# Four of twelve column pairs of a feed-forward's way up as seven half-size products, with the weight sums made by adding transfers

## The chip, the cores and the metric

The kernel runs on one core of one Trainium2 chip. Its five engines work side by side, each through its own queue in order: TensorE (PE in the profile; its weight loads are the row PEld) multiplies, VectorE (DVE) and ScalarE (ACT) do elementwise work and empty PSUM, the accumulators that TensorE writes, GpSimd (POOL) and SyncE (SP) here mostly issue transfers (DMAs) between the main memory (HBM) and SBUF, the working memory. The metric is the device time of one execution in microseconds (us), the median over the runs of a kernel.

## The reference

One batch, 512 tokens, width 1024, two layers, float32. Layer 0 mixes tokens by dilated window attention (24 heads in three groups), layer 1 by a gated linear recurrence (RG-LRU). Each is followed by a gated feed-forward with a causal convolution over three tokens, and each sub-layer is wrapped in two RMS norms.

```python
def conv_ffn(x, w_up, conv_w, conv_b, w_down):
    u = causal_dwconv(x @ w_up, conv_w, conv_b)
    g, v = u[..., :D_FF], u[..., D_FF:]
    return (jax.nn.gelu(g, approximate=True) * v) @ w_down

for layer in range(DEPTH):                     # DEPTH = 2, D_FF = 3072
    h = rms_norm(x, norm_mix_pre[layer])
    h = dilated_attention_mixer(h, ...) if layer % 2 == 0 else rglru_mixer(h, ...)
    x = x + rms_norm(h, norm_mix_post[layer])
    h = rms_norm(x, norm_ffn_pre[layer])
    h = conv_ffn(h, ffn_w_up[layer], ffn_conv_w[layer], ffn_conv_b[layer], ffn_w_down[layer])
    x = x + rms_norm(h, norm_ffn_post[layer])
```

## The kernel before

**Numbers in two parts.** Every large product takes both operands as a rounded high part and the rest, the low part, and is made of three matmuls: high by high, high by low, low by high (`mm3`, line 326). A weight piece is split by one ACT copy (`hi`, line 215, in `pump`) and one DVE subtraction (`lo`, line 226, in `low_parts`). The normed activations stand transposed in `hT`: a high and a low tile of 128 partitions x 8 blocks of features x 512 tokens.

**Weights.** `plan` lists all weight pieces in the order of use. `loads` issues the next one on SP's queue as long as fewer than `RAW_BUFS` = 3 raw buffers of 1 MB are in use (`load`, line 253). `pump` takes the next piece of a landed or coming load and splits it, as long as fewer than `W_UNITS` = 8 split pieces are live; the low part of the previous piece follows the high part of the next, and the last low part of a load frees its raw buffer. `tick` is called after each output tile; it runs the waiting side steps (norms, softmax steps) and the pump. So the program order of every engine is fixed when the kernel is built, by these ticks.

**A feed-forward.** `ffn` walks over 12 pairs of column blocks. For pair j, `feat_tiles` makes two tiles of 128 gate columns and two of 128 value columns, each 8 feature blocks x 3 matmuls over 512 tokens, so a pair is 96 matmuls and 2 MB of weights. Pair 0 runs in token halves, 192 matmuls over 256 tokens. `sink` empties a tile: `conv` makes the first tap on ACT (line 600) and two on DVE (line 604); a gate tile goes through gelu on ACT (line 615), a value tile is multiplied into it on DVE (line 619). `rows_run` then makes the way down token tile by token tile into accumulators, and starts for each finished tile the two norms, `postnorm` (which updates the residual `xs_sb[t]`) and `prenorm` (which makes the next `hT`).

**Half-size products that are there already.** In the attention the value columns of the second and third head group are made by seven products of half size (`value_steps`) in place of eight: sums of corners of `hT` (`sums`, lines 739 to 745, one set for each of two groups of columns) times sums of quarters of the weights (`added`, line 236, on DVE, from raw buffers that are held meanwhile), combined on DVE (line 788).

**GpSimd's queue** loads the bias strips (`toe`, line 666), the norms' gains (line 160) and the small column constants (`columns`, line 551). The gains' tile (`gain`) is also the place of the weight sums. The residual x keeps four tiles of the tag `x` through the whole layer, beside the token sums in the attention.

Of the kernel before, what the change touches and what calls it, by code (L numbers as in the profile page):

```python
# [18 lines left out]
P = 128  # L19
# [14 lines left out]
RAW_BUFS = 3  # L34
# [3 lines left out]
WARM = 14  # L38

# [46 lines left out]
def kernel(  # L86
# [61 lines left out]
    def load_x(t, cuts=1):  # L148
        xt = htp.tile([P, D], F32, tag="x", name=nm("x"), bufs=4)
        n = D // cuts  # L150
        for i in range(cuts):
            c = slice(i * n, (i + 1) * n)
            nc.sync.dma_start(xt[:, c], x[0, t * P : (t + 1) * P, c])
        return xt
# [13 lines left out]
    state = {"dma": 0, "cv": 0, "live": 0, "next": 0, "read": 0, "rows": False, "hold": False}  # L168
# [3 lines left out]
    total = {}  # L172

    def parts_of(kind, raw):

        if kind == "feat":
            return [raw[:, :, m * P : (m + 1) * P] for m in range(2)]
        if kind == "held":
            total["held"] = raw
            return []  # L180
        if kind in ("value", "sum0", "sum"):
            return [raw[:, 2 * i : 2 * i + 2, :] for i in range(2)]
        if kind == "rows":
            return [raw[:, i : i + 1, :] for i in range(2)]
        return [raw]

    def pump(limit=2, now=False):

        for _ in range(limit):
# [4 lines left out]
            if pieces and state["live"] < W_UNITS:  # L194
                i, j, raw = pieces.pop(0)
                last = not pieces
                if plan[i][0] in ("sum0", "sum"):
                    raw = added(plan[i][0], j, raw)
                    if last:
                        state["read"] += 1 + (plan[i][0] == "sum0")  # L200
                        last = False
# [3 lines left out]
                if i < 2 or now:  # L205
# [7 lines left out]
                    state["read"] += last  # L213
# [10 lines left out]
    def low_parts():  # L224
        for _, _, lo, raw, hi, last in late:
            nc.vector.tensor_tensor(lo, raw, hi.bitcast(F32), op=ALU.subtract)  # L226
            state["read"] += last
        late.clear()

    def added(kind, j, raw):  # L230

        if kind == "sum0" and j == 0:
            total["sum"] = cp.tile([P, 4, 512], F32, tag="gain", name=nm("sum"))
        h = slice(2 * j, 2 * j + 2)
        part = total["sum"][:, h, :]
        nc.vector.tensor_tensor(part, total["held"][:, h, :] if kind == "sum0" else part, raw, op=ALU.add)
        return part

    def loads():
        while state["dma"] < len(plan) and state["dma"] - state["read"] < RAW_BUFS:  # L240
            load()

    def load():
        i = state["dma"]
        kind, kd, cols, srcs = plan[i]
        raw = wp.tile([P, kd, cols], F32, tag="raw", name=nm("raw"), bufs=RAW_BUFS)
        at = 0
        for src, n in srcs:
            if i < 2:
                for k in (0, 2):  # L250
                    nc.sync.dma_start(raw[:, k : k + 2, :], src[:, k : k + 2, :])
            else:
                nc.sync.dma_start(raw[:, :, at : at + n] if kd == 4 and cols == 512 else raw[:, at : at + n, :], src)
# [9 lines left out]
    def take(i, j):  # L263
        while (i, j) not in units:
            before = state["live"]
            pump(1, True)
            assert before != state["live"]
# [51 lines left out]
    def w_rows(w, r0):  # L319
        plan.append(("rows", 2, D, [(w[r0 : r0 + 256, :].rearrange("(k p) c -> p k c", p=P), 2)]))  # L320
# [109 lines left out]
    def norms(t, banks, post_g, pre_g, hT):  # L430
        state["hold"] = t >= 2
        postnorm(t, banks, post_g, hT is None)
        if hT is not None:
            yield from prenorm(t, hT, pre_g, 3 if t == 3 else 4)
        if t == 3:
            state["hold"] = False

# [10 lines left out]
    def feat_tiles(n, hT, sink, halves=False):  # L448
# [15 lines left out]
        for c in range(n):  # L464
            i = chunk()
            for m in range(2):
# [4 lines left out]
                tick()  # L471

    def rows_proj(nchunks, act, order, post, pre):
# [12 lines left out]
        def run():  # L486
            return rows_run(nchunks, A, prep, seq, order, post, pre)
# [3 lines left out]
    def rows_run(nchunks, A, prep, seq, order, post, pre):  # L491
# [7 lines left out]
        for tiles, chunks in order:  # L499
            for c in chunks:  # L500
# [9 lines left out]
                for n, part in enumerate(loop):  # L510
# [17 lines left out]
                    for t in tiles:  # L528
                        if left[t] == [0, 0]:
                            side(norms(t, banks[t], post_g, pre_g, hT))  # L530
# [14 lines left out]
    def columns(parts):  # L545
# [4 lines left out]
        for src, c in parts:  # L550
            nc.gpsimd.dma_start(st[at : at + c, :P], src)
# [43 lines left out]
    def ffn(layer, hT, post, pre):  # L595
# [13 lines left out]
        gv = []  # L609

        def sink(b, ps, j):
            m = b % 2
            if b < 2:
                u = conv(ps, 2 * j + m)
                nc.scalar.activation(u, u, AF.Gelu_apprx_tanh)  # L615
                gv.append(u)
# [3 lines left out]

        order = [([0, 1, 2, 3], range(9)), ([0], range(9, 12)), ([1], range(9, 12))]
# [9 lines left out]
    def attention(hT, post, pre):  # L631
# [84 lines left out]
        def sums(n):  # L716

            def cut(i, j, h):
                return hT[h][:, 4 * i : 4 * i + 4, j * 256 : (j + 1) * 256]

            made, run = {}, []
            terms_of = {
                3: [((1, 1), 1), ((0, 1), -1)],
                2: [((0, 0), 1)],
                4: [((1, 0), -1)],
                1: [((0, 1), 1), ((0, 0), -1)],
            }

            def make(*names):
                for name in names:  # L730
                    if name in (3, 1):
                        run[:] = [gp.tile([P, 4, 256], F32, tag="run", name=nm("run"), bufs=1)]
                    hi, lo = (htp.tile([P, 4, 256], F32R, tag="x", name=nm("T"), bufs=4) for _ in range(2))
                    made[name] = hi, lo
                    r = run[0]
                    parts = [(cut(*ij, x).bitcast(F32), sg) for ij, sg in terms_of[name] for x in range(2)]
                    if name in (3, 1):
                        (a, _), (b, _) = parts[:2]
                        nc.vector.tensor_tensor(r, a, b, op=ALU.add)
# [577 lines left out]
```

## Time and profile before

| | |
|---|---|
| median of 3 runs | 1480.87 us (1480.69 to 1481.19) |
| the profiled execution | 1480.85 us, with a span of 1479.1 us from its first to its last instruction |
| engines busy in the span | PE 99%, DVE 58%, ACT 42%, POOL 2% |
| granted TensorE clock, mean | 0.997 |
| DMA | 174.40 MB, mean 118 GB/s |
| matmuls | 7049 |

The page gives for each engine the time in which one of its instructions ran. Matmuls overlap in the pipeline, so the length of one in a group (some 390 ns over 512 columns) is not its price; the price is the distance from one to the next. The view of windows adds up busy time within stretches, the view of waits says what ended the idle time of an engine, and the chain of waits is followed back from the last instruction to whatever released it. "SPq" is SP's queue.

### The profile page before, as it was taken

The page shows a single profiled execution, that of the slowest core. Times are in us where ns is not written, and L with a number is a line of the kernel's source. Part 1 is how long each engine was busy: PE and PEld are TensorE (multiplying, and loading weights), DVE is VectorE, ACT ScalarE, POOL GpSimd, SP SyncE. Part 2 cuts the span into 40 slices and gives each one's busy share as a digit, 9 for nine tenths or more (in the row PEclk, how much of TensorE's full clock was granted, in tenths as well). Part 3 has the DMA queues.
Part 4 walks back from the last instruction along what each step waited for, and adds up shares of the span by engine and source line. Part 5 has one row for each costly group of instructions (what it writes and reads, how often), then busy time and mean ns, then how long its engine had stood idle before and what let it go on. Part 6 is the DMA issues. An engine that isn't in the chain of part 4 may idle for free.

```text
span 1479.1 us, 17722 instructions
## 1 busy us (share of the span) xinstructions
PE 1466.7 (99%) x7049; PEld 1232.1 (83%) x7049; DVE 856.0 (58%) x1459; ACT 623.2 (42%) x1042; POOL 34.2 (2%) x67
## 2 busy tenths in 40 slices
PE   8999999999999999999999999999999999999998
PEld 6788888888888898888888888988898888888886
DVE  5366746684455676555565337778775555565333
ACT  5344333343435453334344234579453333333221
POOL 0121000000000000000000000000000000000000
PEclk9999999999999999999999999999999999999999
DMA  6545354636326143232223321341323232323201
GB/s 224 202 174 166 120 177 158 202 127 223 107 90 217 35 137 114 86 110 90 93 107 116 112 86 44 100 143 57 123 92 114 87 113 86 105 95 121 107 0 57
DMA packets 129714, 174.40 MB, mean 118 GB/s; under 512 B 5775, under 2 KB 108391, under 8 KB 129632
## 3 DMA queue, kind: packets, MB, share of 16 engines
q1 hardware_dynamic: 124736, 162.02, 32.7%
q0 software_dynamic: 4896, 11.26, 2.3%
q8 instruction: 55, 0.90, 0.3%
q14 instruction: 27, 0.22, 0.1%
HBM read 164.82 MB, written 13.14 MB: 120 GB/s over the span
## 4 chain that ended last, share of the span: by engine, by line
PE 97%; DVE 1%; DMA 1%; ACT 1%; SPq 0%; issue 0%; DVEq 0%
PE ps L326 59%; PE acc L326 23%; PE vq L757 5%; PE v L697 3%; PE gate L326 1%; PE tr L375 1%; PE S L932 1%; PE O L903 1%; PE S L868 1%; DMA raw<-in_attn_w_qkv_dram 1%; PE O L1000 1%; PE PT L890 0%; PE PT L981 0%; DVE wlo L226 0%; ACT L L920 0%; PE OT L1004 0%
## 5 line engine op out<-in xcount | busy, mean ns | idle before, releaser
L326 PE MATMUL ps<-hT,whi 128*128 128x512 f32 (+1 forms) x2752 | 802.0, 376 | 0.0
L326 PEld LDWEIGHTS ps<-hT,whi 128*128 128x128 f32 x2752 | 502.7, 188 | 93.1 <-ACT qk L677 0.6
L326 PE MATMUL ps<-hT,wlo 128*128 128x512 f32 (+1 forms) x1376 | 515.2, 374 | 0.0
L226 DVE TENSOR_TENSOR wlo<-raw,whi 128x1024 fp32r<-128x1024 f32 x244 | 295.5, 1219 | 130.0 <-ACT whi L215 129.5
L215 ACT ACTIVATE whi<-raw 128x1024 fp32r<-128x1024 f32 x244 | 253.2, 1052 | 136.6 <-PE acc L326 124.4
L326 PEld LDWEIGHTS ps<-hT,wlo 128*128 128x128 f32 x1376 | 259.0, 188 | 46.4
L604 DVE SCALAR_TENSOR_TENSOR u<-ps,cols,u 128x511 f32<-128x511 f32 x192 | 143.8, 749 | 217.1 <-ACT u L600 213.7
L326 PE MATMUL acc<-whi,ahi 128*128 128x512 f32 x512 | 200.4, 391 | 0.0
L326 PE MATMUL acc<-whi,alo 128*128 128x512 f32 x512 | 199.3, 389 | 0.0
L326 PE MATMUL acc<-wlo,ahi 128*128 128x512 f32 x512 | 199.2, 389 | 0.0
L600 ACT ACTIVATE u<-ps,cols 128x512 f32<-128x512 f32 x96 | 74.8, 779 | 220.0 <-PE ps L326 215.6
L326 PEld LDWEIGHTS acc<-whi,alo 128*128 128x128 f32 x512 | 96.1, 188 | 20.1
L326 PEld LDWEIGHTS acc<-wlo,ahi 128*128 128x128 f32 x512 | 96.2, 188 | 19.6
L326 PEld LDWEIGHTS acc<-whi,ahi 128*128 128x128 f32 x512 | 96.1, 188 | 19.6
L615 ACT ACTIVATE u<-u 128x512 f32<-128x512 f32 x48 | 30.4, 633 | 79.6 <-DVE u L604 79.6
L421 DVE TENSOR_TENSOR post<-acc,gain 128x512 f32<-128x512 f32 x32 | 21.8, 687 | 42.4 <-ACT junk L333 42.4
L677 ACT ACTIVATE qk<-ps 128x512 f32<-128x512 f32 x24 | 14.2, 593 | 71.4 <-PE ps L326 71.4
L855 DVE CUSTOM_DVE_ANT_0 L<-S,toe 128x128 f32<-128x128 f32 (+1 forms) x96 | 25.2, 320 | 30.4 <-PE S L868 14.7
L697 PE MATMUL v<-whi,hT 128*128 128x512 f32 x128 | 42.3, 410 | 0.3 <-ACT hT L379 0.3
L333 ACT ACTIVATE junk<-acc 128x512 f32<-128x512 f32 x32 | 19.0, 596 | 56.0 <-PE acc L326 56.0
L757 PE MATMUL vq<-whi,T 128*128 128x512 f32 x128 | 41.2, 393 | 0.0
L679 DVE COPY qk<-ps 128x512 f32<-128x512 f32 x24 | 16.5, 689 | 35.1 <-PE ps L326 35.1
(197 smaller groups left out, 1184.5 us busy)
## 6 DMA issues: line engine op xcount, KB each, us to landing
raw<-in_ffn_w_up_dram SPq DMA_DIRECT2D x48, 1024.0 KB, 5.2
raw<-in_attn_w_qkv_dram SPq DMA_DIRECT2D x26, 1024.0 KB, 5.1
raw<-in_ffn_w_down_dram SPq DMA_DIRECT2D x24, 1024.0 KB, 4.9
raw<-in_attn_w_qkv_dram SPq DMA_DIRECT2D x40, 512.0 KB, 4.5
raw<-in_lru_w_in_dram SPq DMA_DIRECT2D x8, 1024.0 KB, 5.4
skew<-rowv POOLq DMA_DIRECT2D x3, 1536.0 KB, 12.0
vp<-vrows SPq DMA_DIRECT2D x16, 256.0 KB, 7.4
raw<-in_attn_w_o_dram SPq DMA_DIRECT2D x4, 1024.0 KB, 4.9
```

Source lines behind the costliest of these rows:

```text
L215: nc.scalar.activation(hi, raw, AF.Copy)
L226: nc.vector.tensor_tensor(lo, raw, hi.bitcast(F32), op=ALU.subtract)
L326: mm(dst, l[a], r[b], start=start and n == 0, stop=stop and n == 2)
L333: nc.scalar.activation(junk, h, AF.Square, accum_out=ss[:, i : i + 1])
L421: nc.vector.tensor_tensor(u[i], banks[i], gh[i], op=ALU.mult)
L600: nc.scalar.activation(u, ps, AF.Identity, scale=cc[:, j : j + 1], bias=cc[:, 48 + j : 49 + j])
L604: nc.vector.scalar_tensor_tensor(u[:, d:], ps[:, : S - d], wc, u[:, d:], op0=ALU.mult, op1=ALU.add)
L615: nc.scalar.activation(u, u, AF.Gelu_apprx_tanh)
L679: nc.vector.tensor_copy(dst, src)
L697: mm(banks[t], hT[a][:, k, t * P : (t + 1) * P], W[b][:, k % 2, :], start=(k, a, b) == (0, 0, 0), stop=(k, a, b) == (KD - 1, 1, 0),)
L757: mm(banks[u], act(a)[:, 2 * j + k, u * P : (u + 1) * P], W[b][:, k, :], start=(j, k, n) == (0, 0, 0), stop=(j, k, n) == (1, 1, 2),)
L855: nc.vector.tensor_tensor_reduce(dst, ps, bias, scale=1.0, scalar=3 * NEG, op0=ALU.add, op1=ALU.max, accum_out=mx)
```

## The change

In each feed-forward, pairs 2, 4, 6 and 8 are made by seven products, each interleaved with the ordinary pair that follows it (3, 5, 7, 9). With the features cut in two (k halves 0 and 1), the tokens in two halves and the pair's columns in its first and second half f, one product is one 512 x 256 quarter (or sum of quarters) of the weights times one corner (or sum of corners) of `hT`: 2 x 4 x 3 = 24 matmuls over 256 tokens into one PSUM bank. The combinations are made on DVE into four SBUF tiles, which then go through the same convolution and gelu as other tiles (`ends`).

- *Token sums* are made once per `hT` (`token_sums`) into eight tiles of the tag `x`, in half-tiles on DVE and ACT; in the attention both groups of value columns now use one set.
- *Weight sums* are made in the `gain` tile by chains of transfers (`add_up`): the first quarter by a plain load on SP, the others added to it by loads that GpSimd issues. A feed-forward has two chains of 512 KB, the attention one of 1 MB. The last of a chain is split like any piece, and then the chain's buffer is open for the next one. DVE's additions (`added`) go.
- *Loads*: two raw buffers instead of three; the recurrence's gate weights and the rows of its output weight go into tiles of the tag `x`, which has eight tiles now. Loads stay in the order of the plan, so a chain that isn't open holds those behind it.
- *The residual* is stored to HBM after each mixer's `postnorm` and loaded again before the way down.
- The small column constants are loaded by SP instead of GpSimd, and GpSimd's descriptor scratch is 4096 instead of 8192.

```diff
-RAW_BUFS = 3
+RAW_BUFS = 2
+SLOTS = {"gate": 1, "pair": 2}
+CHAINS = {"first": 0, "sum": 0, "first1": 1, "add1": 1, "sum1": 1}
+PAIRS = [(0, None), (1, None), (3, 2), (5, 4), (7, 6), (9, 8), (10, None), (11, None)]
+WIDE_STEPS = (1, 2, 2, 2)
...
     def loads():
-        while state["dma"] < len(plan) and state["dma"] - state["read"] < RAW_BUFS:
+        while state["dma"] < len(plan):
+            kind = plan[state["dma"]][0]
+            if kind in CHAINS:
+                full = total["busy"][CHAINS[kind]] or not total["open"]
+            elif kind in SLOTS:
+                full = state["slots"] < SLOTS[kind]
+            else:
+                full = state["dma"] - state["read"] >= RAW_BUFS
+            if full:
+                break
             load()
+
+    def add_up(i, kind, cols, srcs):
+
+        first, n = kind.startswith("first"), CHAINS[kind]
+        if total["sum"] is None:
+            total["sum"] = cp.tile([P, 512 // cols, 4, cols], F32, tag="gain", name=nm("sum"))
+        part = total["sum"][:, n]
+        at = 0
+        for src, m in srcs:
+            dst = part[:, :, at : at + m]
+            if first:
+                nc.sync.dma_start(dst, src)
+            else:
+                nc.gpsimd.dma_start(dst, src, accum_op=ALU.add)
+            at += m
+        raws[i] = part
+        total["busy"][n] = kind.startswith("sum")
+        state["read"] += 1
+        state["dma"] += 1
...
+        def sevenths(j):
+            outs = {}
+            def product(piece, act, *then):
+                W = take(*piece)
+                q = psum("vq")
+                for n in range(2):
+                    for k in range(4):
+                        mm3(
+                            q[:, n * 256 : (n + 1) * 256],
+                            [w[:, k, n * P : (n + 1) * P] for w in W],
+                            [act(a)[:, k, :] for a in range(2)],
+                            k == 0,
+                            k == 3,
+                        )
+                done()
+                return q
...
+            duo = chunk()
+            q = product((duo, 0), corner(hT, 0, 0))
+            nc.scalar.activation(c, q, AF.Copy)
+            yield
+            chunk()
+            q = product((chunk(), 0), total_of(3))
+            tt(y, c, q, op=add)
+            yield
+            q = product((duo, 1), corner(hT, 1, 0))
+            out(0, 0, c, q, add)
+            yield
+            chunk()
+            chunk()
+            q = product((chunk(), 0), total_of(2))
+            tt(y, q, y, op=sub)
+            tt(c, q, c, op=sub)
+            yield
+            q = product((chunk(), 0), total_of(4))
+            out(1, 0, y, q, sub)
+            yield
+            q = product((chunk(), 0), corner(hT, 1, 1))
+            tt(c, q, c, op=sub)
+            yield
+            chunk()
+            q = product((chunk(), 0), total_of(1))
+            out(1, 1, y, q, add)
+            out(0, 1, c, q, sub)
...
-        for j in range(12):
+        for j, wide in PAIRS:
             if j == 11:
                 prep(3)
-            feat_tiles(2, hT, lambda b, ps: sink(b, ps, j), j == 0)
+            if j == 1:
+                side(make(TOKEN_PACE))
+            steps = sevenths(wide) if wide else None
+            at = iter(WIDE_STEPS if wide else (0, 0, 0, 0))
...
+            def between():
+                for _ in range(next(at)):
+                    next(steps, None)
+                    tick()
+            feat_tiles(2, hT, sink, j == 0, between)
+        for t in range(4):
+            xs_sb[t] = load_x(t, src=spill[t])
...
+    def quarters_of(w, j, part):
+        def q(kind, i, f, rows=512):
+            srcs = [w[i * 512 : i * 512 + rows, g * D_FF + j * 256 + f * P :][:, :P] for g in range(2)]
+            plan.append((kind, rows // P, 256, [(r.rearrange("(k p) c -> p k c", p=P), P) for r in srcs]))
+        if part == 0:
+            q("duo", 0, 0, 1024)
+            q("first", 0, 0)
+            q("sum", 0, 1)
+            return
+        q("first1", 0, 0)
+        q("add1", 0, 1)
+        q("sum1", 1, 1)
+        q("one", 1, 1)
+        q("sum1", 1, 0)
+        q("first", 0, 1)
+        q("sum", 1, 1)
```

In the plan, `quarters_of` part 0 stands between an ordinary pair's gate load and its value load, part 1 behind the value load.

More of the change, by code (lines that the diff above doesn't have):

```diff
@@ L167 @@
     plan = []
-    state = {"dma": 0, "cv": 0, "live": 0, "next": 0, "read": 0, "rows": False, "hold": False}
+    state = {"dma": 0, "cv": 0, "live": 0, "next": 0, "read": 0, "rows": False, "hold": False, "slots": 4}
     raws, units, pieces = {}, {}, []
     sides, first_tiles = [], []
-    total = {}
+    total = {"busy": [False, False], "open": True, "sum": None}
     def parts_of(kind, raw):
@@ L714, in values @@
                 tick()
[L716 to L739, printed above, removed]
-                        parts = parts[2:]
-                    for a, sg in parts:
-                        nc.vector.tensor_tensor(r, r, a, op=ALU.add if sg > 0 else ALU.subtract)
-                    nc.scalar.activation(hi, r, AF.Copy)
-                    yield 1
-                    nc.vector.tensor_tensor(lo, r, hi.bitcast(F32), op=ALU.subtract)
-                    yield 1
-            return made, make
         def product(banks, act):
```

216 lines of the change are left out of this document (146 added, 70 removed).

## The prediction

> **What bounds the kernel now.** I read the page first, then the chain of waits in order of time, then the groups of instructions, the waits and windows inside the first way up, and last the DMA issues.
>
> ```profile
> span 1479.1 us, 17722 instructions
> PE 1466.7 (99%) x7049; PEld 1232.1 (83%) x7049; DVE 856.0 (58%) x1459; ACT 623.2 (42%) x1042; POOL 34.2 (2%) x67
> ```
>
> TensorE (PE) is busy for all but 12.4 us of the span. The chain of waits says what that busy time is made of (start, length, what, count):
>
> ```profile
> 523.84 5.75 PE ps L326 x48
> 534.21 253.77 PE ps L326 x1176
> 988.63 43.52 PE ps L326 x192
> 1087.84 253.77 PE ps L326 x1176
> ```
>
> The two long pieces are the two ways up, each unbroken: nothing but matmuls ends there. The other two give the price of one matmul in a stream. The piece at 988.63 holds only matmuls over 512 columns: 43.52/192 = 226.7 ns. The piece at 523.84 holds only matmuls over 256 columns: 5.75/48 = 119.8 ns; I use 120. Check: 11 pairs of 96 wide matmuls and 120 narrow ones left of pair 0 give 1056 x 0.2267 + 120 x 0.120 = 253.8 us, as the row says. So a way up has the length of its matmuls, and VectorE (DVE) and ScalarE (ACT) follow it:
>
> ```profile
> 534.00:788.00 254.00, 254.00 (x1179) 212.88 (x1178) 145.06 (x172) 102.59 (x127) 0.00 (x0) 1.00 0.31 102
> 1360.00:1400.00 40.00, 40.00 (x178) 33.10 (x178) 13.68 (x16) 11.06 (x14) 0.00 (x0) 1.00 0.24 82
> DVE u L604 <- ACT u L600: 104.8, 45, 2.8
> SPq L253 <- DVE wlo L226: 261.3, 25, 17.6
> ```
>
> The first two are windows (length, then busy us of PE, weight loads, DVE, ACT, POOL, clock, DMA share, GB/s): one way up, and a piece of the last way down. In the way up DVE is 57% busy, ACT 40%, the DMA engines 31%; the granted clock is 1.00. The other two are waits of that stretch (us, times, longest): DVE idles on ACT, and SyncE's queue (SP) is always held by the low part that frees a raw buffer. Loads are paced by use, not by bandwidth.
>
> **Removed from PE.** A pair is 96 matmuls over 512 columns, 96 x 0.2267 = 21.76 us. In seven products it is 7 x 24 = 168 over 256 columns, each with its own weight load as at 523.84, 168 x 0.120 = 20.16 us. Four pairs in each of two layers: 8 x 1.60 = **12.8 us** less. One eighth of the multiplying would be 21.8 us; the narrow matmul's 120 ns, against half of 226.7, takes back 8 x 168 x 0.0067 = 9.0. The operands keep their forms (128x128 weights, 256 contiguous moving columns), so I take the row without a spread.
>
> The Trainium skill (TensorE: Matmul & The Clock Gate, Back-to-back issue gap) gives 518 cycles for 512 columns and 262 for 256, 216 and 109 ns at full clock. By it the saving would be 19.0 us, an estimate; the rows above are dearer for both and decide.
>
> **Added to DVE and ACT**, all beside the matmuls:
>
> ```profile
> L226 DVE TENSOR_TENSOR wlo<-raw,whi 128x1024 fp32r<-128x1024 f32 x244 | 295.5, 1219 | 130.0 <-ACT whi L215 129.5
> L215 ACT ACTIVATE whi<-raw 128x1024 fp32r<-128x1024 f32 x244 | 253.2, 1052 | 136.6 <-PE acc L326 124.4
> L604 DVE SCALAR_TENSOR_TENSOR u<-ps,cols,u 128x511 f32<-128x511 f32 x192 | 143.8, 749 | 217.1 <-ACT u L600 213.7
> L600 ACT ACTIVATE u<-ps,cols 128x512 f32<-128x512 f32 x96 | 74.8, 779 | 220.0 <-PE ps L326 215.6
> L615 ACT ACTIVATE u<-u 128x512 f32<-128x512 f32 x48 | 30.4, 633 | 79.6 <-DVE u L604 79.6
> L619 DVE TENSOR_TENSOR u<-u,u 128x512 f32<-128x512 f32 x48 | 33.2, 693 | 1.6
> ```
>
> An ordinary pair costs DVE 4 low parts (4.9), 8 taps (6.0) and 2 products (1.4): 12.3 us of 21.76, which is the window's 57%. A pair in sevenths has 7 low parts (8.5), the same taps and products (7.4), 4 combinations over 512 columns (2.8) and 8 over 256. Those have no row: half of 0.69 to all of it; from 0.69 for 512 and 1.22 for 1024, 0.43, so 3.4. Together 22.1. An ordinary pair and one in sevenths, interleaved, are then 34.4 us of DVE in 4 x 5.44 + 7 x 2.88 = **41.9 us** of PE, 82%. ACT: 4 and 7 high parts, 8 first taps, 4 gelus, a copy: 11.6 + 6.2 + 2.5 + 0.6 = 20.9, half. The token sums cost DVE 28 operations over 512 columns, 19.3 us once in each way up, beside pair 1 and the first double pair, where DVE falls some 8 us behind. By the order of the code, eight unit slots put the split of a weight piece 14 to 20 us of PE time ahead of its use, and eight PSUM banks hold some 25 us. I call 14 us **the cover**. Cost while DVE stays inside it: 0. In the attention DVE loses the weight sums and half of the token sums, under a full PE: 0.
>
> **The transfers.** A pair in sevenths reads eleven 512 KB quarters instead of 2 MB, in 512 B runs; five are added on the way by transfers that GpSimd (POOL) issues.
>
> ```profile
> raw<-in_ffn_w_up_dram SPq DMA_DIRECT2D x48, 1024.0 KB, 5.2
> raw<-in_attn_w_qkv_dram SPq DMA_DIRECT2D x40, 512.0 KB, 4.5
> skew<-rowv POOLq DMA_DIRECT2D x3, 1536.0 KB, 12.0
> toe<-skew POOLq DMA_DIRECT2D x16, 64.0 KB, 2.1
> L666 POOL DMA_DIRECT2D toe<-skew x24: 534/537/585, 68.3 to 454.9; - x24
> ```
>
> Bandwidth first. By the windows 1 KB runs move at 102/0.31 = 329 GB/s of full share, 50 ns a run on one of 16 engines, and 4 KB runs at 82/0.24 = 342, 192 ns; a line through both gives 26 ns for 512 B. Per double pair: 2048 runs of 1 KB (6.4 us), 6144 plain ones of 512 B (10.0), and 5120 adding ones, at 26 ns if adding is free and 52 if the old value is fetched like a second run (8.3 or 16.6). That is 25 to 33 us of 41.9: the DMA share rises from 0.31 to 0.6 or 0.8, and still fits.
>
> The length L of one adding quarter, from issue to landing, matters more. No row shows it. Below, it is the plain 512 KB load, 4.5 us; above, the three skew copies, 12.0 us: also issued by POOL, and also 1024 runs. It is a weight load from HBM into SBUF, so I take the near end and add the second fetch, 64 runs per engine x 26 ns = 1.7: **6.2 us**.
>
> What waits for L: the second chain's buffer takes a first load, two additions, a split, a third addition, a split, and only then the next pair's. SP holds that next first load behind a 1 MB load that needs a raw buffer (only two now). One round: 1 MB and first load landing 7 (5.2 and 64 x 26 ns), 2L, split 2.3 (1.05 and 1.22), L, split 2.3, then DVE's work up to the low part that frees the raw buffer (3 low parts, 2 narrow and 2 wide combinations, 4 taps, a product: 9.6). That is 21.2 + 3L against 41.9: even at L = 6.9. Behind a late addition ACT's next high parts and gelus queue, behind ACT the DVE, and behind both PE's weights and banks, 14 us later. With three rounds a layer the loss is 3 x (3L - 20.7) - 14 = 9L - 76 us a layer where positive: 0 up to 8.4, 64 us for both at 12. At 6.2: 0.
>
> The Trainium skill (SBUF — State Buffer, A bandwidth-pool intuition that's wrong) speaks against moving sums to POOL: its descriptors wait while VectorE holds the shared port, 620 ns becoming 3100. By this, the trace does not agree: its longest issue above is 585 ns. Rival 2 works the same mechanism out from rows.
>
> In the **attention** the adding quarters are 1 MB, taken as 8.5 us (5.2 + 64 x 50 ns), and by the order of the code ACT asks for two of each four only one 5.4 us tile after they may start. ACT is held some 3 us, four times in all; its weights are needed 20 us later, but softmax steps queue behind it. I take 1 us on PE, with bounds of 0 and 4 x 3 = 12.
>
> **Moved.** Thirteen small constant loads go from POOL to SP, 0.4 us of issue each: 5 us of a queue that otherwise waits. The residual is stored and read back (2 MB each way per FFN), ordered after work that SP already waits for: 0. Two raw buffers for three: a landing of 5.2 us against 10.9 us of matmuls for each 1 MB in ordinary stretches: 0. The cover for these is the eight unit slots; without it each late load would cost up to 5.2 us.
>
> **The sum** against this execution's own 1480.85 us (span 1479.1 and 1.75 around it; the runs' median is 1480.87): -12.8 + 1 = 1469. I forecast **1469 us**; this case's own range is 1466.5 to 1474.
>
> **Rivals.**
> (1) *The adding chain decides: slower.* Place: the second chain in pairs 4, 6 and 8; point: net loss from 2 x (9L - 76) = 12.8, L = 9.2 us. For it: the skew row, a DMA share near 0.8 in which transfers delay each other, ACT's strict order. Against it: the plain row's 4.5 us. At L = 10, 28 - 12.8: 1496; at 12, 1532.
> (2) *POOL's issue is held by DVE.* If POOL could write its descriptors only in DVE's idle time, 18% of a double pair, the 0.54 us of an issue would become 3.0; two a quarter make L 6.2 + 4.9 = 11.1 and the time 1480.85 - 12.8 + 2 x 23.9 = 1516. Against it: the 585 ns maximum above, with DVE at 57%, where that rule would give 1.25 us.
> (3) *DVE becomes the bound.* If each of a double pair's 8 tiles still costs DVE a wait for ACT: with 0.78 us (L600) it is 34.4 + 6.2 = 40.6, hidden; with all of 104.8/45 = 2.3 it is 52.8. Halfway, 46.7: 4 x 4.8 - 14 = 5.2 a layer, 1479. Against it: those waits are mostly for PE and shrink when DVE is late.
> (4) *Nothing to tell*: attention's 12 us eat the gain, 1480.
>
> **Chances.** Forecast 0.58; (1) 0.18; (2) 0.04; (3) 0.12; (4) 0.08. What a measurement can tell from no change is 0.2%, 3 us. Faster: the forecast and some of (3) and (4), 0.63; same 0.12; slower 0.25. The range, 1466 to 1505, holds the forecast, (3), (4) and (1) up to L of about 10.5.
>
> **What would show it.** In the after-profile: the way up's matmuls at 120 ns; each way up about 6.4 us shorter, as one unbroken piece; DVE near 0.8 in the double pairs; adding issues landing under 8 us; no PE wait on a high or low part of a sum. Wrong would be: landings above 9 us, and PE idle before products of pairs 4, 6, 8 (rival 1); POOL issues in us (2); DVE full with PE waiting on it (3); PE idle between 100 and 480 us (4).

## The result, and the profile after

The changed kernel takes 1521.86 us (median of 4 runs, 1517.82 to 1527.11) against 1480.78 (1480.44 to 1481.19): the ratio is 1.0279, with a 95% interval of 1.0241 to 1.0317. It is slower by 41 us where I forecast 12 us faster, and outside the range. The profiled execution took 1524.97 us, with a span of 1523.2.

First the page of the changed kernel: span, engines, and the shares of the chain of waits by engine.

```profile
span 1523.2 us, 19481 instructions
PE 1473.3 (97%) x7625; PEld 1261.5 (83%) x7625; DVE 924.8 (61%) x1619; ACT 652.7 (43%) x1090; POOL 150.3 (10%) x147
...
PE 60%; DMA 14%; DVE 10%; issue 7%; ACT 6%; POOL 2%; SPq 1%; DVEq 0%; ACTq 0%; POOLq 0%
```

PE is idle for 50 us instead of 12, and it is also busy for longer (1473.3 for 1466.7 us) although it has less to multiply. The chain of waits, nearly all PE in the two long pieces of before, now runs through transfers, DVE and ACT. By the starts of the first matmul of each stage:

| stage (us) | before | after | difference |
|---|---|---|---|
| to the end of the attention | 523.8 | 533.1 | +9.3 |
| way up, layer 0 | 264.0 | 280.2 | +16.2 |
| way down, layer 0 | 132.5 | 132.5 | 0 |
| recurrence | 157.2 | 159.2 | +2.0 |
| way up, layer 1 | 264.0 | 280.8 | +16.8 |

These make 44.3 of the 44.1 us between the two spans. The ways up were to become 6.4 us shorter each and became 16 longer. Windows of the changed kernel (columns as in the prediction: length, busy us of PE, weight loads, DVE, ACT, POOL, clock, DMA share, GB/s):

```profile
533.00:813.00 280.00, 264.87 (x1552) 236.39 (x1551) 202.71 (x285) 124.18 (x165) 52.49 (x42) 0.98 0.68 150
640.00:660.00 20.00, 14.51 (x83) 12.79 (x82) 8.64 (x12) 6.75 (x9) 5.14 (x4) 0.91 0.79 143
660.00:700.00 40.00, 39.24 (x239) 34.88 (x238) 26.38 (x35) 16.11 (x21) 9.91 (x9) 1.00 0.73 156
700.00:720.00 20.00, 15.85 (x91) 14.62 (x91) 16.47 (x22) 10.52 (x13) 5.50 (x5) 0.83 0.94 163
```

In the way up PE is idle for 15.1 us. The losses sit in bursts: around 650 and 703 it idles for 5.5 and 4.2 us of 20, between them for 0.8 of 40 (a third burst lies at 750). In the bursts the granted clock falls too. A window of 20 us at 0.91 has 3.4 us at half speed, one at 0.83 has 6.8; this way up has 13.6 us at half speed in all. Half of that, 6.8 us, is PE time lost besides the idling, and 15.1 + 6.8 is the whole distance of 22 us to a way up without waits (257.9, below).

The chain of waits from 640 to 720 us shows what PE waited for (start, length, what):

```profile
653.56 5.16 DMA sum<-in_ffn_w_up_dram
658.76 0.04 issue
658.85 0.92 issue
659.77 1.05 ACT whi L220
660.82 0.67 ACT u L701
661.51 0.76 DVE u L705
...
667.47 1.22 DVE wlo L231
668.71 0.37 SPq L300
669.08 0.05 issue
669.18 8.50 DMA sum<-in_ffn_w_up_dram
677.68 0.39 issue
678.08 5.85 DMA sum<-in_ffn_w_up_dram
683.93 0.39 issue
684.32 4.78 DMA sum<-in_ffn_w_up_dram
```

This is the round of the prediction, closed on itself: an adding transfer (653.56, the second half of the first chain's addition, which GpSimd issues right behind the second chain's third), ACT's and DVE's work up to the low part that frees a raw buffer, SP's 1 MB load at 668.71, right behind it the next pair's first load of the second chain (669.18, 8.5 us), the first addition (678.08), the second (684.32). GpSimd's timeline gives its length, from third addition to third addition (a row of three holds the two transfers of a third addition and the first half of the first chain's addition behind it):

```profile
648.82 3.87 POOL L270 DMA_DIRECT2D sum<-in_ffn_w_up_dram  x3 [11.25 <-DVE wlo L231]
...
678.08 2.56 POOL L270 DMA_DIRECT2D sum<-in_ffn_w_up_dram  x2 [10.73 <-DMA sum<-in_ffn_w_up_dram]
684.32 1.28 POOL L270 DMA_DIRECT2D sum<-in_ffn_w_up_dram  x1 [3.69 <-DMA sum<-in_ffn_w_up_dram]
686.06 1.28 POOL L270 DMA_DIRECT2D sum<-in_ffn_w_up_dram  x1 [0.46 <-issue]
697.80 3.86 POOL L270 DMA_DIRECT2D sum<-in_ffn_w_up_dram  x3 [10.46 <-DVE wlo L231]
```

That is 49.0 us here (the four third additions, at 598.0, 648.8, 697.8 and 747.4, are 49.8 apart on average) against the 41.9 us of PE in a double pair. Three rounds overrun by 3 x 7.9 = 24 us; the way up lost 22.

### The profile page after: what moved, and what is told of

Same layout as the page of the kernel before. It is cut to its first block, busy times and chain, and to the rows that moved or that the text cites. A ratio compares the mean times of both kernels' runs of the same rounds, so it can differ in the third digit from the quotient of the medians.

```text
span 1523.2 us, 19481 instructions
## 1 busy us (share of the span) xinstructions
PE 1473.3 (97%) x7625; PEld 1261.5 (83%) x7625; DVE 924.8 (61%) x1619; ACT 652.7 (43%) x1090; POOL 150.3 (10%) x147
## 3 DMA queue, kind: packets, MB, share of 16 engines
q0 software_dynamic: 55072, 40.39, 16.9%
## 4 chain that ended last, share of the span: by engine, by line
PE 60%; DMA 14%; DVE 10%; issue 7%; ACT 6%; POOL 2%; SPq 1%; DVEq 0%; ACTq 0%; POOLq 0%
PE ps L377 25%; PE acc L377 21%; DMA sum<-in_ffn_w_up_dram 11%; PE vq L903 5%; DVE wlo L231 3%; PE v L877 2%; DVE u L705 2%; POOL sum L270 2%; ACT whi L220 2%; PE vq L377 1%; DVE xb L1241 1%; PE tr L426 1%; PE O L1037 1%; PE S L1066 1%; ACT u L701 1%
## 5 line engine op out<-in xcount | busy, mean ns | idle before, releaser
L377 PE MATMUL ps<-hT,whi 128*128 128x512 f32 (+1 forms) x2240 | 645.8, 373 | 0.0
L377 PEld LDWEIGHTS ps<-hT,whi 128*128 128x128 f32 x2240 | 405.1, 189 | 71.4 <-ACT qk L857 0.8
L377 PE MATMUL ps<-hT,wlo 128*128 128x512 f32 (+1 forms) x1120 | 415.7, 371 | 0.0
L231 DVE TENSOR_TENSOR wlo<-raw,whi 128x1024 fp32r<-128x1024 f32 x236 | 285.7, 1219 | 133.0 <-ACT whi L220 132.5
L270 POOL DMA_DIRECT2D sum<-in_ffn_w_up_dram x80 | 103.0, 1534 | 556.5 <-DMA sum<-in_ffn_w_up_dram 417.2
L231 DVE TENSOR_TENSOR wlo<-sum,whi 128x1024 fp32r<-128x1024 f32 x48 | 58.4, 1222 | 113.5 <-ACT whi L220 113.2
L705 DVE SCALAR_TENSOR_TENSOR u<-ps,cols,u 128x511 f32<-128x511 f32 (+1 forms) x128 | 95.8, 748 | 51.5 <-ACT u L701 49.2
L377 PEld LDWEIGHTS acc<-whi,ahi 128*128 128x128 f32 x512 | 96.1, 188 | 21.2 <-ACT ahi L170 1.9
L377 PE MATMUL vq<-T,wlo 128*128 128x256 f32 x256 | 78.8, 308 | 29.2 <-DVE wlo L231 29.2
L377 PE MATMUL vq<-T,whi 128*128 128x256 f32 x512 | 102.6, 300 | 1.6 <-ACT whi L220 1.6
L377 PEld LDWEIGHTS vq<-T,whi 128*128 128x128 f32 x512 | 88.1, 209 | 4.2 <-ACT whi L220 3.4
L377 PE MATMUL vq<-hT,whi 128*128 128x256 f32 x384 | 70.0, 283 | 0.0
```

The lines of the kernel that those rows point to most:

```text
L270: nc.gpsimd.dma_start(dst, src, accum_op=ALU.add)
L377: mm(dst, l[a], r[b], start=start and n == 0, stop=stop and n == 2)
L705: nc.vector.scalar_tensor_tensor(u[:, d:], ps[:, : S - d], wc, u[:, d:], op0=ALU.mult, op1=ALU.add)
```

## The experiments

All start from the changed kernel unless said otherwise. Ratios are to the kernel before, on the same chip.

**1. The constants.** The small column constants go back to GpSimd, as before.

```diff
-            nc.sync.dma_start(st[at : at + c, :P], src)
+            nc.gpsimd.dma_start(st[at : at + c, :P], src)
```

> The changed kernel with the thirteen small constant loads back on POOL's queue. Theory A (the attention's extra 9.2 us come from these loads on SP: PE idles 4.8 us for one of them and then runs 6.8 us at half the granted clock, 3.4 us): about 8 us less than the changed kernel's 1522, so 1513 to 1515, with the first way up starting near 525 instead of 533 us. Theory B (the attention's own adding chain holds ACT): unchanged, 1520 to 1525.

1525.87 us (1.0306, 1.0290 to 1.0321), 0.9 above the range of theory B and far from that of A. The attention ends at 534.2, the ways up take 278.1 and 281.6. On GpSimd the constants stand behind the first adding transfer of the attention, and PE waits for them longer than on SP (6.6 us for 4.8). Moving them back alone gains nothing. That does not clear the constants, as runs 9 to 11 show.

**2. No sevenths in the feed-forwards.**

```diff
-PAIRS = [(0, None), (1, None), (3, 2), (5, 4), (7, 6), (9, 8), (10, None), (11, None)]
+PAIRS = [(j, None) for j in range(12)]
...
-            if j == 1:
-                side(make(TOKEN_PACE))
```

> The changed kernel with all twelve pairs of both ways up ordinary (no products of half size and no chains there); attention, recurrence, loads and the stored residual as changed. If the ways up lose by their chains or products, both are back at 264.2 us and the total is 1480.8 + 9.2 (attention) + 2.0 (recurrence) = 1492. If two raw buffers or the stored residual cost in the ways up, they stay longer than 264.2 and the total lies above 1495.

1491.14 us (1.0072, 1.0057 to 1.0087), as expected if the ways up lose by their chains or products. The ways up are 264.0 each, exactly as before, with two raw buffers; the attention ends at 533.9 and the recurrence takes 158.8. So about 10 us of the loss are the attention's, under 2 the recurrence's, and the rest comes with the sevenths.

**3. Copies in place of additions.** GpSimd's transfers in the feed-forwards overwrite the chain's buffer instead of adding to it. The weight sums are left out, so the numbers are not the reference's; every instruction and byte from HBM stays.

```diff
-                nc.gpsimd.dma_start(dst, src, accum_op=ALU.add)
+                nc.gpsimd.dma_start(dst, src, **({"accum_op": ALU.add} if cols == 512 else {}))
```

> The changed kernel, but the feed-forwards' adding transfers only copy (the weight sums are left out: the last quarter overwrites). Same bytes, same issues, same waits. If the fetch of the old value is what makes a quarter land late, landings fall from 5.7 us a transfer to under 4.5, the round of the second chain from 49.6 to near 42, each way up from 280 to 258 to 266, total 1480 to 1495. If it is the order of issues and waits, the round stays above 47 and the total above 1510.

1480.10 us (0.9996, 0.9986 to 1.0005), and both ways up take **257.9 us**: 6.1 less than before, where 6.4 was forecast. The products, DVE's added work and the token sums are all in it and cost PE nothing. Its window, then GpSimd's transfers of the weight sums in this kernel, by tile (ns of issue: least, median, most) and by DMA issue (size, median us to landing):

```profile
534.00:792.00 258.00, 258.00 (x1553) 231.42 (x1553) 203.47 (x287) 125.00 (x167) 30.88 (x42) 1.00 0.55 165
```

```profile
L270 POOL DMA_DIRECT2D sum<-in_ffn_w_up_dram x80: 747/747/768, 566.9 to 1272.1; - x80
sum<-in_ffn_w_up_dram POOLq DMA_DIRECT2D x80, 256.0 KB, 4.2
```

The same two views of the changed kernel:

```profile
L270 POOL DMA_DIRECT2D sum<-in_ffn_w_up_dram x80: 1258/1286/2393, 565.3 to 1324.7; - x80
sum<-in_ffn_w_up_dram POOLq DMA_DIRECT2D x80, 256.0 KB, 5.7
```

Adding costs 0.54 us more of GpSimd's time for each transfer and 1.5 us more to its landing. GpSimd's queue moves the same 40.39 MB in 19232 packets here and in 55072 in the changed kernel, 448 fewer for each of the 80 transfers that no longer add. DVE is equally busy in both (203 us), so the longer issue comes with the addition.

**4. No chains.** Each product gets one plain quarter through the two raw buffers; all weight sums of the feed-forwards are left out.

```diff
-        q("first1", 0, 0)
-        q("add1", 0, 1)
-        q("sum1", 1, 1)
+        q("one", 0, 1)
...
-        q("first", 0, 1)
-        q("sum", 1, 1)
+        q("one", 1, 1)
```

> The changed kernel, but each product of the ways up multiplies one plain quarter, loaded into a raw buffer (the weight sums are left out): 3.5 MB a pair instead of 5.5 and no chain; products, token sums, splits and combinations as changed. If the chains are the cause: both ways up at 257.8 us, total 1480.8 - 12.8 + 11.2 = 1479. If VectorE's 82 per cent with its waits for ScalarE paces the double pairs: ways up still above 270, total above 1503.

1529.37 us (1.0323, 1.0306 to 1.0340), ways up 280.5 and 279.2: as slow without any addition. The time lies in the range that was given for VectorE as the pace; but in run 3 VectorE has the same work and PE never waits, so that reading falls. In the first way up SP's queue waits 231.8 us, 40 times, for the low parts that free raw buffers, and PE stops three times, 15.7 us in all. As I read it, two raw buffers that each hold only a quarter run dry as the chains did; this run put another late load in the place of the chains and does not price them. What it has in common with the changed kernel is loads that stand on SP behind a raw buffer's release; experiment 6 takes that from the second chain.

**5. The attention's chain opened later**, after the bias constants and the fourth local head's strip.

```diff
-    total = {"busy": [False, False], "open": True, "sum": None}
+    total = {"busy": [False, False], "open": False, "sum": None}
...
             toeplitz(T, 0, h, 256)
+            if h == 3:
+                total["open"] = True
```

> The changed kernel with the weight-sum chain of the attention opened only after the bias constants and the fourth local head's bias strip have been put into POOL's queue (so no adding transfer stands ahead of them); the way up is untouched. Theory Q (order in POOL's queue: the adding transfer waits 14.7 us for its first load at 108.6 and the strips stand behind it): the 13.4 us wait of VectorE for the strip goes, the attention's end falls from 533.1 back to about 524 to 526 and the half-speed clock at 122.9 is gone; both ways up stay at 280; total 1511 to 1515 us. Rival T (the traffic of the chain itself, 1 MB per quarter beside the 1536 KB of the skewed copies, makes everything late): the strips land late wherever they stand in the queue, the attention still ends at 530 to 533, total 1519 to 1523.

1516.49 us (1.0244, 1.0229 to 1.0259): 1.5 us above the range of theory Q. The attention ends at 525.0, 8.1 earlier; no stop of PE and no half-speed clock there. But opening the chain later moved its first load on SP too, from 96 to 115 us, so this does not tell queue order from traffic; runs 9 to 11 do.

**6. The second chain started earlier.** In the plan, `first1` and `add1` go ahead of the pair's `duo` (and the product steps skip chunks in the new order).

```diff
         if part == 0:
+            q("first1", 0, 0)
+            q("add1", 0, 1)
             q("duo", 0, 0, 1024)
...
-        q("first1", 0, 0)
-        q("add1", 0, 1)
         q("sum1", 1, 1)
```

> The changed kernel with one move in the way up: the second chain's first load and first addition (first1, add1) stand ahead of the pair of corners (duo) in the order of loads instead of behind the gate's weights, so that SP issues them when the chain's buffer is read and not behind a load that waits for one of the two raw buffers. Theory O (order: in the changed kernel the chain's buffer was free at 657.6 and its next first load was issued at 669.2, behind a raw load that had waited for a VectorE remainder; the round from third addition to third addition was 49.6 us): the round falls by 8 to 11 us to 38.6 to 41.6, below the 41.9 us of PE; each way up falls from 280 to between 258 and 266; total 1480 to 1494 us. Rival R (the rate at which adding transfers move is the limit: the DMA engines show 78% to 106% of share while they run): the round stays at 48 to 50 us, total 1518 to 1524.

1481.64 us (1.0004, 0.9994 to 1.0013): 40 us less for two lines moved. The ways up take 259.1 and 257.9, with every addition made. Theory R falls: the DMA engines carry the same bytes in less time, and it is not their rate that limited. The third additions of the first way up are now 44.6, 40.9 and 41.9 us apart, with 41.9 us of PE in between. So either repair is enough by itself: shorter transfers (run 3) or an earlier start of the chain.

**7. Three sevenths pairs, wider apart.**

```diff
+PAIRS = [(0, None), (1, None), (3, 2), (4, None), (6, 5), (7, None), (9, 8), (10, None), (11, None)]
```

> The changed kernel with three sevenths pairs in each way up instead of four, an ordinary double pair's worth of PE between them (63.7 us of PE from one sevenths pair to the next instead of 41.9); the chain's order is the changed kernel's. Theories O and R alike make the round 49.6 us, which now fits: each way up is 264.0 less three savings of 1.5 us, 259 to 262 us, plus what the first pair's late chain costs; total 1480 to 1490 us. Rival C (adding transfers slow the other engines while they run, whether or not anyone waits for them): each sevenths pair keeps its loss of 4 us over an ordinary one, each way up is 274 to 278 us, total 1510 to 1518.

1495.33 us (1.0096, 1.0079 to 1.0113), above the range that O and R share and below that of C. The ways up take 265.9 and 262.3. The waits of PE for weights that are left:

```profile
PE vq L377 <- DVE wlo L231: 6.7, 3, 2.4
```

The third additions are now 66 and 69 us apart, with 63.7 us of PE in between. So the round is not a fixed 50 us that fits into a longer gap: its loads are issued when the plan reaches them, and the chain of waits still runs through a chain's first load (9.9 us from 634.7, then the addition at 645.0). Space between the pairs does not help what is late inside one.

**8. Both: chain opened later, second chain earlier** (the edits of 5 and 6).

> Both edits together: the attention's chain opened after the bias strips, and first1 with add1 ahead of duo in the way up. If theories Q and O both hold, their gains add: 9 us in the attention and 18 to 22 us in each way up off 1522, so 1469 to 1486 us, which is faster than the kernel before if the ways up reach 262 or less. If only Q holds 1511 to 1515; if only O holds 1480 to 1494.

**1473.82 us**, 0.9954 of the kernel before (0.9939 to 0.9969): the gains add. Page, window and GpSimd's timeline of the first way up:

```profile
span 1470.8 us, 19466 instructions
PE 1455.1 (99%) x7625; PEld 1248.6 (85%) x7625; DVE 926.3 (63%) x1619; ACT 651.9 (44%) x1090; POOL 150.4 (10%) x147
```

```profile
526.00:784.00 258.00, 258.00 (x1554) 231.41 (x1553) 203.29 (x285) 123.56 (x165) 52.80 (x42) 1.00 0.73 163
```

```profile
635.34 3.89 POOL L270 DMA_DIRECT2D sum<-in_ffn_w_up_dram  x3 [14.12 <-DVE wlo L231]
...
655.50 3.88 POOL L270 DMA_DIRECT2D sum<-in_ffn_w_up_dram  x3 [5.08 <-DVE wlo L231]
662.69 1.29 POOL L270 DMA_DIRECT2D sum<-in_ffn_w_up_dram  x1 [3.30 <-issue]
676.86 3.88 POOL L270 DMA_DIRECT2D sum<-in_ffn_w_up_dram  x3 [12.88 <-DVE wlo L231]
```

PE does not stop once in the way up. The DMA engines are busier than in the changed kernel (0.73 for 0.68) and GpSimd issues the same additions in the same 3.9 us. Third additions are 41.5 us apart, which is PE's own pace, and there is slack: the second addition's last transfer is issued at 662.69 and landed at 668.3, and ACT reads it at 674.2, where in the changed kernel ACT started at 695.08, 0.02 us after the landing. The third addition waits for that split.

**9. Only the attention's additions held back**; the chain's first load stays at 96 us.

```diff
                 full = total["busy"][CHAINS[kind]] or not total["open"]
+                full = full or kind == "sum" and not total["adds"]
...
             toeplitz(T, 0, h, 256)
+            total["adds"] |= h == 3
```

> The changed kernel where only the adding transfers of the attention's chain are held back until the fourth local head's bias strip is in POOL's queue; the chain's first load stays where the change has it (SP, about 96 us), so its megabyte still shares the DMA engines with the skewed copy. Theory Q (order in POOL's queue alone): the strips are issued at about 95 and land at about 106 to 109, VectorE does not wait 13.4 us for them, the attention ends at 524 to 527, total 1511 to 1517. Rival T (the chain's traffic): the first load beside the skewed copy still makes strips and constants late, the attention ends at 529 to 533, total 1518 to 1522. The kernel that opened the whole chain later moved both, and could not tell these apart.

1521.31 us (1.0276, 1.0261 to 1.0292): **theory Q falls**. The time lies in the range of rival T, but of what T would make late the strips are not: they are issued at 95.9 and 96.5 and land at 107.0 and 107.5 (before, the first landed at 107.5), VectorE's wait of 13.4 us for them is gone, and the attention still ends at 532.6. PE stopped for something else, here and in the changed kernel. The longest wait of PE from 90 to 240 us, first of the changed kernel, then of this one:

```profile
PE cols L655 <- DMA st<-in_ffn_conv_w_dram: 4.8, 1, 4.8
```

```profile
PE cols L656 <- DMA st<-in_lru_lambda_dram: 4.1, 1, 4.1
```

It is the transposes of the column constants (`st`), which the change moved to SP. SP's timeline and the window in the changed kernel:

```profile
112.77 2.35 SPq L652 DMA_DIRECT2D st<-in_lru_conv_w_dram  x4
...
118.82 0.27 SPq L652 DMA_DIRECT2D st<-in_lru_lambda_dram  x1
119.19 1.24 SPq L652 DMA_DIRECT2D st<-in_ffn_conv_w_dram  x3
```

```profile
110.00:120.00 10.00, 8.61 (x47) 7.15 (x45) 0.00 (x0) 1.19 (x2) 4.07 (x6) 1.00 1.13 257
```

They are issued from 113 to 123 us, in the middle of the adding transfers of 109 to 121, with the DMA engines' share above 1. Before, GpSimd issued the first of them at 97.22. Run 8 fits: there SP issues them as late (from 113.2), but the first addition starts at 120.1, and PE does not stop for them.

**10. As 9, with the second chain earlier.**

> The kernel with first1 and add1 ahead of duo, and the adding transfers of the attention's chain (not its first load) held back as above. Theory Q with theory O: 1471 to 1476 us, the same as where the whole chain was opened later (1473.8) or 1 to 2 us less, since the sum is ready earlier. Rival T: 1478 to 1482, as with first1 and add1 moved alone (1481.6).

1477.78 us (0.9975, 0.9964 to 0.9987), between the two ranges: the stop at the constants is there but shorter (3.4 us), and the attention ends at 530.5.

**11. As 10, constants on GpSimd again**, those of the recurrence ahead of the first addition (the edits of 1, 6 and 9).

> The kernel with first1 and add1 early and the attention's adding transfers held back to the fourth head's strip, and now the thirteen small column constants issued by GpSimd again: those of the recurrence stand ahead of the first adding transfer in POOL's queue, those of the feed-forwards right behind it. Theory K (what stops TensorE at about 119 is neither the strip nor the queue as such, but the transposes of the constants, whose loads were issued at 113 to 119 and landed late among the adding transfers of 111 to 122): the stop at the recurrence's constants goes, one at the feed-forwards' constants may take its place; the attention ends between 525 and 530, total 1472 to 1478. Rival F (the chain's first megabyte beside the skewed copy is the cause, wherever the constants stand): the stop of 4 us and the half-speed clock stay, attention 530 to 533, total 1477 to 1480.

1474.73 us (0.9961, 0.9947 to 0.9975). The attention ends at 525.6, the clock stays at full speed, and the waits of PE from 90 to 240 us are down to these:

```profile
PE O L1039 <- DVE PT L1031: 0.7, 1, 0.7
PE ps L378 <- ACT qk L858: 0.6, 1, 0.6
```

The chain's first load still runs beside the skewed copy, and the DMA share from 100 to 120 us is 0.94 and 1.02 (0.95 and 1.13 in the changed kernel), so theory F falls and K holds: what cost the attention 7.5 of its 9.3 us were the constants, late among the additions.

**12. As 11, additions held back until all thirteen constants are issued.**

```diff
             yield from feature_columns()
+            total["adds"] = True
...
-            total["adds"] |= h == 3
```

> As the kernel with the constants on GpSimd, but the attention's adding transfers are held back until all thirteen constants have been put into POOL's queue (flag at the end of the bias generator instead of the fourth head's strip). Theory K: no stop of TensorE at the transposes, no half-speed clock at 120 to 125, attention ends 523.5 to 526, total 1470 to 1474. Rival F: the stop stays, attention 530 to 533, total 1477 to 1480.

1485.65 us (1.0037, 1.0024 to 1.0049), outside both ranges: no stop at the constants, but the attention ends at 538.6. Another wait of PE took its place. GpSimd's timeline, then PE's waits:

```profile
192.78 2.57 POOL L271 DMA_DIRECT2D sum<-in_attn_w_qkv_dram  x2 [24.00 <-DMA sum<-in_attn_w_qkv_dram]
194.63 1.88 POOL L848 DMA_DIRECT2D toe<-skew  x2
```

```profile
PE O L1039 <- DVE PT L1031: 8.1, 1, 8.1
```

Here an addition stands 24 us at the head of GpSimd's queue, waiting for its chain's first load, and the strips of later heads stand behind it; VectorE waits 16.6 us for one of them, until 201.9, PE waits 8.1 us for the softmax after it, and the granted clock is at half speed for 10.2 us from 206.8. So the mechanism of theory Q exists. The blocking is not new in this run: in the changed kernel an addition waits 27.6 us there and VectorE 16.4 us for a strip, and in run 11 VectorE waits 17.0 us, and each time it costs PE 0.7 us. What differs is when the wait ends: 190.3 in run 11, 201.9 here.

## Why the prediction was wrong, step by step

*The products* (-12.8 us): right. 264.0 to 257.9 is 6.1 for each way up, 12.2 in all (runs 3 and 8). *DVE and ACT hidden*: right; DVE is busy 203 of 258 us (79%) and PE never waits. Rival 3 did not happen.

*The adding chain* (0 us): **wrong, the step that decided.** I had named its round and its loop, and put 21.2 + 3L = 39.8 us against 41.9. Measured in the round shown: the third addition's quarter took 6.4 us until ACT read it (648.8 to 655.3), the next pair's first addition 6.2 until the second could start (678.1 to 684.3), the second 10.8 until ACT read it (to 695.1): 23.4 where 3 x 6.2 = 18.6 was reckoned. One transfer's median of 5.7 lies below my 6.2, but a quarter is two transfers, and the second addition's second half was issued 1.7 us behind the first and took 9.0 to land. ACT's reads of the sums in this round (the second chain's third, the first chain's, the next pair's second):

```profile
655.26 1.06 ACT L220 ACTIVATE whi<-sum 128x1024 fp32r<-128x1024 f32 x1 [3.00 <-DMA sum<-in_ffn_w_up_dram]
658.80 1.06 ACT L220 ACTIVATE whi<-sum 128x1024 fp32r<-128x1024 f32 x1 [2.49 <-DMA sum<-in_ffn_w_up_dram]
...
695.08 1.06 ACT L220 ACTIVATE whi<-sum 128x1024 fp32r<-128x1024 f32 x1 [9.34 <-DMA sum<-in_ffn_w_up_dram]
```

The rest of the round took 25.6 instead of 21.2: SP's 1 MB and first load 9.4 for 7, the splits and DVE's work 16.2 for 14.2. Of these 16.2 us, 2.5 are no work: ACT waits until 658.8 for the first chain's addition, which shares GpSimd's queue and had no term in my round. So L was short by 1.6 and the fixed part by 4.4, and both together make 49.0 of 39.8; with either alone the formula, with its 14 us of cover, would still have given no loss.

*The cover* (14 us to spare): wrong as well. The first stop of PE, at 647, comes after one overrun of 9 us, and of the 24 us of overrun all but 2 arrive at PE. *Half speed after a stop*: not in the sum at all, 6.8 us in each way up.

Rival 1, the adding chain, was the outcome, with its place (the later sevenths pairs) and its sign. Its price was wrong: by its formula 1522 needs L = 11.4, where the quarters took 7.8; it knew nothing of the fixed part's growth or the clock, and it counted on the cover. I gave it 0.18 because I set L from a single plain load and left 2 us of slack in a loop of ten links, each of them bounded from one row. Experiment 6 shows what the estimate should have asked: not only how long the loop is, but where it is entered. `first1` waited on SP behind a load that waited for a raw buffer, until 669.2, when its own buffer had been free since 657.6.

*Rival 2* (DVE holds GpSimd's issue): no. The issues did grow, to 1.29 us, but the rival's rule gave 3.0 for a double pair (its 1.25 was for the DVE share of before), and copies beside an equally busy DVE took 0.747.

*The attention* (+1 us, bounds 0 and 12): 9.3, inside the bounds for another reason. ACT held by the chain was not it. *The moved constants* (0 us): wrong; SP's queue did wait anyway, but the loads were issued 15 us later than on GpSimd and landed among the additions. The 9.3 are 4.8 us of waiting, 3.4 of half speed and 0.7 of waiting for the softmax behind a late strip (run 12); some 0.4 has no name.

*Two raw buffers and the spill* (0 us): no loss in the ways up (run 2). The recurrence is 1.6 to 2.4 us longer in every kernel with the change; 1.0 to 1.8 of it is a PE wait for ACT's split of the recurrence's output (1.5 of 2.0 in the changed kernel). What makes that late was not tried.

Put together, run 8 is the forecast with its mistakes repaired: -12.2 in the ways up, +2.2 left in the attention, +2.0 in the recurrence, -8.0 us in sum, and its span is 8.3 shorter. Run 11 reaches the same by the other repair of the attention. Which of the two is better lies inside their intervals.

## What to carry to other kernels

A loop of transfers, splits and buffer releases has to be laid out with the order of the queues in it: first ask which load starts it and what that load stands behind, and then how long its links are; here two plan entries moved ahead were worth 40 us, and the adding transfers landed no sooner (median 6.3 us in run 6 for 5.7). A sum of ten links, each taken from one row, that fits with 5% to spare is not yet a fit. Small loads that are moved to another queue are priced by the traffic at their new time, and a queue that waits in order (here, an addition waiting for its first load) makes everything behind it late, which costs time when it ends too late for the next user.

## What the runs showed of the hardware

- **An adding transfer is not a copy with an operand more.** 256 KB in runs of 512 B: 1.29 us of issue on GpSimd for 0.75, 5.7 us to landing for 4.2, 448 packets more (changed kernel and run 3). The DMA share of the way up is 0.73 with additions (run 8) and 0.55 with copies (run 3), of the same bytes from HBM in the same 258 us.
- **Stops of about 4 us cost about half as much again.** In the way up shown, each of PE's three stops of 4.1 us came with 3.4 or 6.8 us of granted clock at half speed; the kernel before has none between its start and its end. Stops of about 2 us (run 7) were followed by half speed in some cases and not in others. The Trainium skill (TensorE: Matmul & The Clock Gate, Why this matters for your kernels) says that gaps over about 3 us between bursts of matmuls bring the half rate back, and its Terms give the price as the throttled time times the missing share of the clock: 13.6 x 0.5 = 6.8 us, and PE was busy for 6.9 us more in that way up than in run 8's. The trace agrees for the stops of 4.1 us; in run 7, stops of 1.8 and 2.2 us were followed by 3.4 us of half speed too.
- **Windows with a DMA share above 1.** It is 1.13 from 110 to 120 us of the changed kernel, among adding transfers, and 1.05 from 10 to 20 us of the kernel before, which has none. So the share of a short window is no measure of what is left.
- **What lands behind the skewed copy lands with it.** In run 9, e, back, res and two strips were issued at 94.3 to 96.5, right behind the 1536 KB copy, and landed from 106.1 to 107.5, just after its own landing at 105.1. The Trainium skill (DMA: Bandwidth & Descriptors, SWDGE vs HWDGE vs iDMA) says that GpSimd's transfers have one queue allocated; the order of these landings agrees. It doesn't show the queue to be the cause: the chain's first load, issued on SP's queue at 96.6, had GpSimd wait for it until 111.0.
